# Attention scores by halves of a block: 192 key columns for 64 queries of two heads

## The chip, the core and the metric

The kernel runs on one core of a Trainium2 chip. A core has a matrix engine, TensorE (PE in the profile; PEld is its loading of weights, which overlaps the matmuls), a vector engine VectorE (DVE), an activation engine ScalarE (ACT), GpSimd (POOL), and SyncE (SP), which here issues most of the DMAs. The operands of TensorE come from the on-chip memory SBUF, its results go to banks of PSUM. Each engine works off its own queue of instructions in order; semaphores tie the queues together. The metric is the device time of one execution in microseconds; three executions of the kernel before took 1844.89, 1845.12 and 1846.22 us, so the median is 1845.12 us. The profile is of one further execution of 1844.67 us.

## The reference

Two layers of a decoder trunk on x of 1024 tokens by 1024 channels, in float32. Each layer mixes tokens (attention in a sliding window beside a causal pooling) and then runs a dense SwiGLU network; both are wrapped in norms modulated by a condition c. What matters here is the attention: 8 query heads and 2 key/value heads of 64 channels, blocks of 128 tokens, a window of 128 keys that ends at the query itself, and a sink per head that takes part in the softmax only.

```python
def sliding_window_attention_with_sinks(q, k, v, sinks):
    qb = q.reshape(B, nb, BLOCK, N_KV_HEADS, GROUP, HEAD_DIM)
    ...
    k_cat = jnp.concatenate([jnp.pad(kb, pad)[:, :-1], kb], axis=2)
    v_cat = jnp.concatenate([jnp.pad(vb, pad)[:, :-1], vb], axis=2)
    scores = jnp.einsum("bnqkgd,bnskd->bnkgqs", qb, k_cat).astype(jnp.float32)
    scores = scores * (HEAD_DIM ** -0.5)
    qi = jnp.arange(BLOCK)[:, None]
    kj = jnp.arange(2 * BLOCK)[None, :]
    diff = qi + BLOCK - kj
    ...
    valid = (diff[None] >= 0) & (diff[None] < WINDOW) & (key_abs >= 0)
    scores = jnp.where(valid[None, :, None, None], scores, NEG_INF)
    ...
    probs = jax.nn.softmax(jnp.concatenate([scores, sink], axis=-1), axis=-1)[..., :-1]
    out = jnp.einsum("bnkgqs,bnskd->bnqkgd", probs.astype(v.dtype), v_cat)
```

Query t of a block sees keys t+1 to 127 of the block before and keys 0 to t of its own block: always 128 of 256 (in block 0 only its own). Queries 0 to 63 see nothing of keys 64 to 127 of their own block, and queries 64 to 127 nothing of keys 0 to 63 of the block before.

## The kernel before

**Tiling.** The 1024 tokens are taken in two halves of 512 (T), each of four blocks of 128 (P). In each layer the combined projection comes first: u (for the pooling), q, and k with v, half by half (`u_pass`, `q_pass`, `kv_pass`), then the output projection (`mix_out`) and the feed-forward network. Operands are kept as a rounded high part and a low part (`split`, L223 on ACT for the high and L224 on DVE for the low part), so that a product takes three matmuls (`mm`, L286, is the helper of all of them; `turn`, L291, that of the transposes on TensorE).

**An attention group** is one block and one key/value head, that is 4 query heads: 16 groups per layer, 32 in the program, 4 of them in block 0. A group is a generator (`group` in `attention`) with these steps:

- Keys and queries are split into high and low parts (L1040 and L1041 for the queries), transposed on TensorE into a bank of the pool msc, and copied by ACT to sa (the transposed keys, kT in the code; L1030, L1033) and to qT (L1053, scaled). qT has one buffer.
- `att_scores` runs twice per group (u = 0, 1), each time for two heads into one bank of msc. For each head two matmuls of 256 key columns (kT's two parts) stream past 128 stationary columns, the queries of that head; in block 0 they have 128 columns.
- The 256 keys of a query are folded into 128 slots of S (the tile sb), one slot for a key of the block before or for the key of the own block at the same place: ACT copies the part of the block before (L1072), then DVE overwrites it where the key belongs to the own block's past (`copy_predicated`, L1076, with the mask own, a lower triangle). In block 0 GpSimd fills S with a large negative number in place of ACT's copy. Slot 128 holds the sink.
- The maximum (L1080, DVE), four exps with their sums (L1087, ACT), the reciprocal and the scaling (L1092 and L1093 on ACT, L1096 on DVE).
- `att_probs`: transposes of S on TensorE, split into two pth tiles (L223, L224); GpSimd's `affine_select` (L1112) makes the own block's part of each.
- `att_values`: two matmuls of pth with the difference of the two blocks' values (vz: the older values, dz: the step between blocks), added in the bank pv, and evicted by ACT and DVE (L1129, L1130).

**Order.** TensorE's order is written by hand; that of the other engines is the tile scheduler's. The groups, the pooling (`pool_mix`) and the sums that make the modulation (`ada_flow`, whose DVE part is L611 and L613) are chains woven into the dense matmuls. `weave` runs the main pass and, after each piece, steps the side chain that is due first. Due times count matmul columns issued so far, in steps of 6144 columns (STEP): a group waits LEADS[0] steps after its start, LEADS[1] after the query transposes, and so on; LEADS[4] stands between the transposes of S and the first value matmuls. CLOSE and GAPS space the modulation's sums, and a number in `gate_flow` spaces those of the gate. A dense matmul works in a pool acc of 4 banks; msc has 3, pv 1.

**Names in the prediction.** acc, msc, pv: banks of PSUM. hT: transposed input; hi, lo: the two parts of a weight (or of q and k); raw: a loaded or computed tile ahead of its split (L713 makes the normed input from a bank); uT, pt: the pooling's inputs and sums; cfa, cfb: larger tiles, of the output among others; ada: the modulation's sum; fn: a norm's tile; sk: the sinks.

Of the kernel before, what the change touches and what calls it, by code (L numbers as in the profile page):

```python
# [14 lines left out]
I32 = mybir.dt.int32  # L15
AF = mybir.ActivationFunctionType
ALU = mybir.AluOpType
# [3 lines left out]
P = 128  # L21
S = 1024
D = 1024
DEPTH = 2
NH = 8
NKV = 2
GRP = NH // NKV
HD = 64
# [7 lines left out]
NFF = DFF // P  # L36
NPAIR = NFF // 2
KD = D // P
T = 512
NT = T // P  # L40
NHALF = S // T
# [9 lines left out]
NEG = -1e30  # L51
SCALE = HD ** -0.5
# [16 lines left out]
def hybrid_decoder_kernel(  # L69
# [73 lines left out]
    def msc_bank():  # L143
# [26 lines left out]
        out=own, in_=own, pattern=[[-1, P]], compare_op=ALU.is_ge,  # L170
        fill=0.0, base=0, channel_multiplier=1,
    )

    tpos = const.tile([P, HALO], I32, name="tpos")
    nc.gpsimd.iota(tpos, pattern=[[1, HALO]], base=1, channel_multiplier=0)
# [449 lines left out]

    GATE_BEGIN = 0.0
    GATE_GAP = 1.9
    CLOSE = 1.59
    GAPS = (0.79, 0.51)

    def closing(close, got):
        yield from close(*got) or ()
# [411 lines left out]
    def att_queries_turned(stk):  # L1044

        bank = msc_bank()
        for i in range(GRP):
            turn(
                bank[:, i * P : (i + 1) * P].bitcast(F32R),
                stk[:, i].rearrange("p a d -> p (a d)"), ident_r,  # L1050
            )
        qT = t_("qT", [P, GRP * P], F32R)
        nc.scalar.activation(qT, bank, AF.Copy, scale=SCALE)  # L1053
        return qT

    def att_seen(blk):

        return slice(0 if blk else P, 2 * P)

    def att_scores(blk, u, qT, kT, S):  # L1060

        bank = msc_bank()
        cs = att_seen(blk)
        for ii in range(2):
            dst = bank[:, ii * 2 * P : (ii + 1) * 2 * P][:, cs]
            q = qT[:, (2 * u + ii) * P : (2 * u + ii + 1) * P]
            mm(dst, q, kT[0][:, cs], True, False)
            mm(dst, q, kT[1][:, cs], False, True)
        both = bank.rearrange("p (i o k) -> p i o k", i=2, o=2)
        dst = S[:, 2 * u : 2 * u + 2, 0:P]  # L1070
        if blk:
            nc.scalar.activation(dst, both[:, :, 0, :], AF.Copy)  # L1072
        else:
            nc.gpsimd.memset(dst, NEG)
        seen = own.bitcast(I32).rearrange("p (o k) -> p o k", o=1).to_broadcast([P, 2, P])
        nc.vector.copy_predicated(dst, seen, both[:, :, 1, :])  # L1076

    def att_max(S):
        mx = t_("st", [P, 8])[:, :GRP]
# [21 lines left out]
    def att_probs(blk, S):  # L1101

        bank = msc_bank()
        for i in range(GRP):
            turn(bank[:, i * P : (i + 1) * P], S[:, i, 0:P], ident)
        seen = [t_("pth", [P, 512], F32R) for _ in range(2)]
        split(*seen, bank)
        if not blk:
            return [seen]
        here = [t_("pth", [P, 512], F32R) for _ in range(2)]  # L1110
        for v, r in zip(seen, here):
            nc.gpsimd.affine_select(  # L1112
                out=r.rearrange("p (i q) -> p i q", i=GRP), in_=v.rearrange("p (i q) -> p i q", i=GRP),
                pattern=[[0, GRP], [1, P]], compare_op=ALU.is_ge, fill=0.0, base=0, channel_multiplier=-1,
            )
        return [seen, here]

    def att_values(n, vals, probs, opening, closing, cat, t):

        if opening:  # L1120
            attn["pv"] = ps.tile([P, 512], F32, tag="pv", name="pv", bufs=1)
        pv = attn["pv"]
        both = vals[:, n].rearrange("p o d -> p (o d)")
        mm(pv, both, probs[0], opening, False)
        mm(pv, both, probs[1], False, closing)
        if closing:
            high, low = (pv[o * HD : (o + 1) * HD].rearrange("p (j q) -> p j q", j=GRP) for o in range(2))
            dst = cat[n * HD : (n + 1) * HD, :, t * P : (t + 1) * P]
            nc.scalar.activation(dst, low, AF.Copy)  # L1129
            nc.vector.tensor_add(dst, high, dst)  # L1130

# [2 lines left out]
    def attention(h, qkvs, sink, cat, begin, period):  # L1134

        def group(t, n):
            blk = h * NT + t
            both = t_("sb", [P, D])
            S = both[:, : GRP * SW].rearrange("p (i k) -> p i k", i=GRP)[:, :, : P + 1]
            step = both[:, GRP * SW : GRP * SW + KVW]  # L1140
            keys = None
            if n == 0:
                if t == 0:
                    att_rotary(blk, qkvs[t], both)
                keys = att_keys(blk, qkvs[t])
            queries = att_queries(n, qkvs[t])
            if n == 0 and t + 1 < NT:
                att_rotary(blk + 1, qkvs[t + 1], both)
            if n == 0:
                if blk:  # L1150
                    nc.gpsimd.tensor_sub(step, qkvs[t][:, QK:QKV], attn["raw"])
                attn["raw"] = qkvs[t][:, QK:QKV]
            hs = slice(n * GRP, (n + 1) * GRP)
            nc.gpsimd.tensor_copy(S[:, :, P : P + 1], sink[:, hs].rearrange("p (i o) -> p i o", o=1))
            yield LEADS[0]
            if keys is not None:
                att_keys_turned(blk, keys)
            qT = att_queries_turned(queries)
            yield LEADS[1]
            kT = attn["k", blk]  # L1160
            for u in range(GRP // 2):
                att_scores(blk, u, qT, (kT[:, 2 * n], kT[:, 2 * n + 1]), S)
                if u == 0:
                    yield LEADS[2]
            att_softmax(S, att_max(S), h == 0)
            yield LEADS[3]
            probs = att_probs(blk, S)
            if n == 0:
                used = [attn["v"], att_vals("dz", step)] if blk else []
                attn["v"] = att_vals("vz", qkvs[t][:, QK:QKV])  # L1170
                attn["vals", blk] = used or [attn["v"]]
            parts = list(zip(attn["vals", blk], probs))
            for i, (vals, prob) in enumerate(parts):
                yield LEADS[4 + i]
                att_values(n, vals, prob, i == 0, i == len(parts) - 1, cat, t)

        return Chains([group(t, n) for t in range(NT) for n in range(NKV)], begin, period)

    LEADS = (0.9, 0.85, 0.25, 2.72, 1.2, 0.64)

    POOL_STEPS = len(WINDOWS) + 1

# [420 lines left out]
    def layer_rows(l, d):  # L1603
        bq = t_("bqkv", [P, QKV])
        eng = nc.sync
        eng.dma_start(bq, b_in[l : l + 1, 0:QKV].to_broadcast([P, QKV]))
        sk = t_("sk", [P, NH])
        eng.dma_start(sk, sinks[l : l + 1, :].to_broadcast([P, NH]))
        d["bq"], d["sink"] = bq, sk

    rows0 = load_col_rows(0)
# [74 lines left out]
    for l in range(DEPTH):  # L1686
# [33 lines left out]
        def gate_flow():  # L1720
            if l:
                return
            one, two = ada_gate(l, 0)
            yield from ada_flow([one], [cats[0][1][:, i, :] for i in range(4)], 3.0)
            while 1 not in cats:
                yield 0.5
            yield from ada_flow([two], [cats[1][1][:, i, :] for i in range(4)], 2.11)
# [219 lines left out]
```

## Time and profile before

| | us |
|---|---|
| median of three executions | 1845.12 |
| the profiled execution | 1844.67 |
| its span, first to last instruction | 1843.0 |
| TensorE busy | 1815.0 (98%), 8615 instructions |
| weight loads busy | 1505.1 (82%) |
| VectorE busy | 1500.5 (81%), 2450 instructions |
| ScalarE busy | 949.5 (52%), 1816 instructions |
| GpSimd busy | 76.4 (4%), 144 instructions |

The granted clock of TensorE is 0.999 of full speed on average. The rows below are the busy tenths of 40 equal slices (46 us each) of the span; attention runs in slices 2 to 7 and 21 to 26, where GpSimd works and ScalarE is busiest:

```profile
PE   7999999999999999999999999999999999999998
...
DVE  7799987787888887788976798876877887877687
ACT  4886895563222323445657759855622322344452
POOL 0022110000000000000001202100000000000000
```

The costliest group of attention's matmuls, and the loads of their stationary operand (busy us, mean ns of one, idle time ahead of them and what ended it):

```profile
L286 PEld LDWEIGHTS msc<-sa,qT 128*128 128x128 f32 x256 | 37.9, 189 | 9.3 <-ACT qT L1053 2.4 <-issue 1.6 <-ACT cfb L1195 1.2
L286 PE MATMUL msc<-sa,qT 128*128 128x256 f32 x224 | 36.5, 285 | 2.2 <-ACT qT L1053 1.0 <-DVE pth L224 0.8 <-ACT cfb L1195 0.3
```

Busy times of matmuls overlap, since one starts to stream before the one ahead of it has drained. So 285 ns is not what such a matmul costs; that is read from the distance of starts. Idle time of an engine that is not the bottleneck costs nothing by itself.

### The profile page before, as it was taken

How to read it: one execution, taken by the hardware profiler on the slowest of the kernel's cores; microseconds unless marked ns; L12 is line 12 of the kernel's file. 1: busy time of each engine (PE TensorE's matmuls, PEld its weight loads, DVE VectorE, ACT ScalarE, POOL GpSimd, SP SyncE). 2: the span in 40 equal slices, each digit the busy share in tenths (PEclk: the TensorE clock that was granted, in tenths of full speed). 3: DMA queues.
4: the chain of work that ended last, by engine and by line, in shares of the span. 5: the costliest groups of instructions: out<-in, count | busy, mean ns of one | idle time of the engine just before them, and what ended most of it. 6: DMA issues, size and time to landing. Idle time of an engine off the chain costs nothing.

```text
span 1843.0 us, 25184 instructions
## 1 busy us (share of the span) xinstructions
PE 1815.0 (98%) x8615; PEld 1505.1 (82%) x8615; DVE 1500.5 (81%) x2450; ACT 949.5 (52%) x1816; POOL 76.4 (4%) x144
## 2 busy tenths in 40 slices
PE   7999999999999999999999999999999999999998
PEld 5888888888888888888888888888888888888886
DVE  7799987787888887788976798876877887877687
ACT  4886895563222323445657759855622322344452
POOL 0022110000000000000001202100000000000000
PEclk9999999999999999999999999999999999999999
DMA  9637747764565565844577485567635545574343
GB/s 328 231 114 224 258 158 234 230 215 162 172 205 194 177 217 204 293 160 135 197 262 238 149 251 205 183 208 230 233 131 187 175 168 197 177 274 144 113 141 122
DMA packets 237157, 363.85 MB, mean 197 GB/s; under 512 B 17946, under 2 KB 126418, under 8 KB 237028
## 3 DMA queue, kind: packets, MB, share of 16 engines
q1 hardware_dynamic: 236420, 360.14, 58.9%
q10 hardware_dynamic: 576, 2.10, 0.3%
q8 instruction: 68, 1.11, 0.2%
q14 instruction: 61, 0.50, 0.1%
q0 software_dynamic: 32, 0.00, 0.0%
HBM read 274.60 MB, written 87.57 MB: 197 GB/s over the span
## 4 chain that ended last, share of the span: by engine, by line
PE 87%; ACT 6%; DVE 5%; issue 2%; DMA 1%; DVEq 0%; ACTq 0%; POOL 0%; SPq 0%; POOLq 0%
PE acc L286 80%; PE msc L286 3%; PE msc L291 2%; PE pv L286 1%; ACT raw L713 1%; ACT sb L1087 1%; DVE ada L613 1%; ACT hT L223 1%; DVE lo L224 1%; ACT hi L223 0%; ACT junk L660 0%; ACT uT L975 0%; DMA pos_i<-in_positions_dram 0%; DVE pth L224 0%; DMA cfb<-in_ada_w_dram 0%
## 5 line engine op out<-in xcount | busy, mean ns | idle before, releaser
L223 ACT ACTIVATE hi<-raw 128x1024 fp32r<-128x1024 f32 (+1 forms) x314 | 268.6, 867 | 313.0 <-PE acc L286 171.1
L224 DVE TENSOR_TENSOR lo<-raw,hi 128x1024 fp32r<-128x1024 f32 (+1 forms) x314 | 307.8, 984 | 84.9 <-ACT hi L223 82.5
L286 PE MATMUL acc<-t,hi 128*128 128x512 f32 x1056 | 325.3, 389 | 0.0
L286 PE MATMUL acc<-hT,hi 128*128 128x512 f32 x928 | 287.7, 395 | 0.0
L286 PEld LDWEIGHTS acc<-t,hi 128*128 128x128 f32 x1056 | 198.1, 188 | 41.2
L286 PE MATMUL acc<-t,lo 128*128 128x512 f32 x528 | 205.4, 389 | 0.0
L286 PE MATMUL acc<-bh,hi 128*128 128x512 f32 x520 | 202.9, 390 | 0.0
L286 PE MATMUL acc<-bh,lo 128*128 128x512 f32 x520 | 202.5, 389 | 0.0
L286 PEld LDWEIGHTS acc<-hT,hi 128*128 128x128 f32 x928 | 168.7, 188 | 31.6 <-issue 0.3
L286 PE MATMUL acc<-hT,lo 128*128 128x512 f32 x512 | 187.9, 391 | 0.0
L1396 DVE TENSOR_TENSOR fn<-acc,fn 128x512 f32<-128x512 f32 x176 | 120.5, 685 | 44.4 <-PE acc L286 44.4
L286 PE MATMUL acc<-ph,hi 128*128 128x512 f32 x328 | 126.3, 389 | 0.0
L286 PE MATMUL acc<-t,hT 128*128 128x512 f32 x528 | 123.3, 389 | 0.0
L1311 ACT ACTIVATE sb<-sb 128x512 f32<-128x512 f32 x38 | 24.0, 632 | 181.5 <-DVE sb L1396 157.3
L286 PEld LDWEIGHTS acc<-t,hT 128*128 128x128 f32 x528 | 99.1, 188 | 20.6
L286 PEld LDWEIGHTS acc<-t,lo 128*128 128x128 f32 x528 | 99.1, 188 | 20.5
L286 PEld LDWEIGHTS acc<-bh,hi 128*128 128x128 f32 x520 | 97.6, 188 | 20.2
L286 PEld LDWEIGHTS acc<-bh,lo 128*128 128x128 f32 x520 | 97.6, 188 | 20.2
L286 PEld LDWEIGHTS acc<-hT,lo 128*128 128x128 f32 x512 | 95.6, 188 | 20.0
L286 PE MATMUL acc<-b,hi 128*128 128x512 f32 x352 | 108.4, 389 | 0.0
L223 ACT ACTIVATE bh<-two_b 128x512 fp32r<-128x512 f32 x100 | 62.3, 623 | 71.7 <-PE acc L286 66.4
L286 PE MATMUL acc<-hi,hT 128*128 128x512 f32 (+1 forms) x352 | 97.4, 360 | 0.7 <-ACT hT L223 0.7
(341 smaller groups left out, 3525.5 us busy)
## 6 DMA issues: line engine op xcount, KB each, us to landing
raw<-in_w_gate_dram SPq DMA_DIRECT2D x44, 512.0 KB
raw<-in_w_up_dram SPq DMA_DIRECT2D x44, 512.0 KB
ar<-in_ada_w_dram SPq DMA_DIRECT2D x80, 256.0 KB
raw<-keeps SPq DMA_DIRECT2D x40, 512.0 KB
cfb<-in_ada_w_dram SPq DMA_DIRECT2D x72, 256.0 KB
keeps<-fn SPq DMA_DIRECT2D x66, 256.0 KB
two_b<-in_w_down_dram SPq DMA_DIRECT2D x30, 512.0 KB
raw<-in_w_in_dram SPq DMA_DIRECT2D x52, 256.0 KB
```

The costliest lines, as they stand in the source:

```text
L223: a = nc.scalar.activation(hi, src, AF.Copy)
L224: v = nc.vector.tensor_sub(lo, src, hi.bitcast(F32))
L286: return nc.tensor.matmul(dst, lhs, rhs, start=start, stop=stop)
L291: return nc.tensor.transpose(dst, src, eye_)
L613: ins = nc.vector.scalar_tensor_tensor(acc, w, c_, acc, op0=ALU.mult, op1=ALU.add)
L713: nc.scalar.activation(hf, bank, AF.Identity, bias=shift, scale=scale)
L1087: nc.scalar.activation(S[:, i, :], S[:, i, :], AF.Exp, bias=nm[:, i : i + 1], accum_out=sm[:, i : i + 1])
L1311: nc.scalar.activation(g, g, AF.Silu)
L1396: ins = nc.vector.tensor_add(halves_of(dst)[m], bank, halves_of(src)[m])
```

## The change

The queries in qT are stored by halves of the block: first the queries 0 to 63 of the four heads, then the queries 64 to 127. A stationary operand of 128 columns now holds 64 queries of two heads. Such a half sees at most 192 of the 256 keys, so each score matmul has 192 columns: keys 0 to 191 for the first half, 64 to 255 for the second (in block 0: 64 and 128 columns). Of the three runs of 64 keys in the result, ACT copies two to S (for the second half in reversed order, so that they land in their slots), and DVE's predicated copy has 64 slots per row in place of 128. In block 0 the second half needs an ACT copy of 64 slots that was not there (4 more instructions in the program). A row of S now stands for another head and query, so the sinks are loaded in two DMAs per layer, one for each half of the partitions, and copied to S another way; the select on the probabilities has a pattern of three levels, and the eviction of the values puts the queries back in order. TensorE has as many instructions as before. Four numbers that space the side chains change with it.

```diff
+HP = P // 2
...
+    nc.gpsimd.tensor_copy(own[HP:P, 0:HP], own[HP:P, HP:P])
...
-    CLOSE = 1.59
-    GAPS = (0.79, 0.51)
+    CLOSE = 1.69
+    GAPS = (0.84, 0.51)
...
         qT = t_("qT", [P, GRP * P], F32R)
-        nc.scalar.activation(qT, bank, AF.Copy, scale=SCALE)
+        nc.scalar.activation(
+            qT.rearrange("p (h i t) -> p h i t", h=2, i=GRP),
+            bank.rearrange("p (i h t) -> p h i t", h=2, i=GRP), AF.Copy, scale=SCALE,
+        )
         return qT
...
-    def att_seen(blk):
-
-        return slice(0 if blk else P, 2 * P)
-
     def att_scores(blk, u, qT, kT, S):
 
         bank = msc_bank()
-        cs = att_seen(blk)
-        for ii in range(2):
-            dst = bank[:, ii * 2 * P : (ii + 1) * 2 * P][:, cs]
-            q = qT[:, (2 * u + ii) * P : (2 * u + ii + 1) * P]
+        first = 0 if blk else P if u == 0 else HP
+        for m in range(2):
+            dst = bank[:, m * 2 * P + first : m * 2 * P + 3 * HP]
+            q = qT[:, (2 * u + m) * P : (2 * u + m + 1) * P]
+            cs = slice(u * HP + first, u * HP + 3 * HP)
             mm(dst, q, kT[0][:, cs], True, False)
             mm(dst, q, kT[1][:, cs], False, True)
-        both = bank.rearrange("p (i o k) -> p i o k", i=2, o=2)
-        dst = S[:, 2 * u : 2 * u + 2, 0:P]
+        both = bank.rearrange("p (m o k) -> p m o k", m=2, o=4)
+        dst = S[:, 2 * u : 2 * u + 2, 0:P].rearrange("p m (o k) -> p m o k", o=2)
         if blk:
-            nc.scalar.activation(dst, both[:, :, 0, :], AF.Copy)
+            nc.scalar.activation(dst, both[:, :, 0:2, :] if u == 0 else both[:, :, 1::-1, :], AF.Copy)
         else:
-            nc.gpsimd.memset(dst, NEG)
-        seen = own.bitcast(I32).rearrange("p (o k) -> p o k", o=1).to_broadcast([P, 2, P])
-        nc.vector.copy_predicated(dst, seen, both[:, :, 1, :])
+            nc.gpsimd.memset(S[:, 2 * u : 2 * u + 2, 0:P], NEG)
+            if u:
+                nc.scalar.activation(dst[:, :, 0, :], both[:, :, 1, :], AF.Copy)
+        seen = own[:, 0:HP].bitcast(I32).rearrange("p (o k) -> p o k", o=1).to_broadcast([P, 2, HP])
+        nc.vector.copy_predicated(dst[:, :, u, :], seen, both[:, :, 2, :])
...
             nc.gpsimd.affine_select(
-                out=r.rearrange("p (i q) -> p i q", i=GRP), in_=v.rearrange("p (i q) -> p i q", i=GRP),
-                pattern=[[0, GRP], [1, P]], compare_op=ALU.is_ge, fill=0.0, base=0, channel_multiplier=-1,
+                out=r.rearrange("p (h i t) -> p h i t", h=2, i=GRP),
+                in_=v.rearrange("p (h i t) -> p h i t", h=2, i=GRP),
+                pattern=[[HP, 2], [0, GRP], [1, HP]], compare_op=ALU.is_ge, fill=0.0, base=0, channel_multiplier=-1,
             )
...
-            hs = slice(n * GRP, (n + 1) * GRP)
-            nc.gpsimd.tensor_copy(S[:, :, P : P + 1], sink[:, hs].rearrange("p (i o) -> p i o", o=1))
+            last = S[:, :, P : P + 1].rearrange("p (h m) o -> p h (m o)", h=2)
+            nc.gpsimd.tensor_copy(last, sink[:, n : n + 1, :].to_broadcast([P, 2, 2]))
...
-    LEADS = (0.9, 0.85, 0.25, 2.72, 1.2, 0.64)
+    LEADS = (0.9, 0.85, 0.25, 2.72, 1.13, 0.64)
...
-        sk = t_("sk", [P, NH])
-        eng.dma_start(sk, sinks[l : l + 1, :].to_broadcast([P, NH]))
+        sk = t_("sk", [P, NH // 2])
+        for i in range(2):
+            eng.dma_start(sk[i * HP : (i + 1) * HP, :], sinks[l : l + 1, i:NH:2].to_broadcast([HP, NH // 2]))
+        sk = sk.rearrange("p (n m) -> p n m", n=NKV)
...
-            yield from ada_flow([one], [cats[0][1][:, i, :] for i in range(4)], 3.0)
+            yield from ada_flow([one], [cats[0][1][:, i, :] for i in range(4)], 2.82)
```

The numbers and the lighter copies shift the orders at some places. In the changed kernel lines stand two to seven further down (L224 becomes L226, L286 L288, L291 L293, L1076 L1080, L1080 L1084). A row names line, operation, output and inputs, and the shape of the output.

On VectorE, in the q projection of layer 0's second half (about 121 to 127 us of the span), before:

```order
L1076 COPY_PREDICATED sb<-own,msc 128x2x128
L1005 TENSOR_TENSOR vz<-qkv,vz 128x2x64
L1076 COPY_PREDICATED sb<-own,msc 128x2x128
L224 TENSOR_TENSOR pth<-msc,pth 128x512
L1080 TENSOR_REDUCE st<-sb 128x4
L1014 TENSOR_TENSOR hi<-qkv,hi 128x2x128
L1041 TENSOR_TENSOR hi<-qkv,hi 128x4x64
L224 TENSOR_TENSOR lo<-raw,hi 128x512 x2
```

The same place now:

```order
L1084 TENSOR_REDUCE st<-sb 128x4
L547 TENSOR_TENSOR ar<-msc,ar 1x512
L1232 TENSOR_TENSOR pt<-pt,rcnt 128x16
L548 TENSOR_TENSOR ar<-ar 1x512
L226 TENSOR_TENSOR lo<-raw,hi 128x512
L1094 RECIPROCAL st<-st 128x4
L1007 TENSOR_TENSOR vz<-qkv,vz 128x2x64
L1100 TENSOR_TENSOR sb<-sb,st 128x2x128
L226 TENSOR_TENSOR lo<-raw,hi 128x512
```

The two low parts of a weight stood together behind the split of probabilities and the low parts of keys and queries; now the first of them stands right behind the maximum of the group before, and those rows come after it.

On TensorE, at the second group of block 0 (about 81 to 85 us), before:

```order
L286 MATMUL msc<-sa,qT 128x128 x4
L291 MATMUL msc<-ident,sb 128x128 x4
L286 MATMUL acc<-hT,hi 128x512 x2
L286 MATMUL acc<-hT,lo 128x512
L286 MATMUL msc<-sa,qT 128x128 x4
L291 MATMUL msc<-ident,cfb 128x128 x4
```

And now:

```order
L293 MATMUL msc<-ident,sb 128x128 x4
L288 MATMUL msc<-sa,qT 128x64 x4
L288 MATMUL acc<-hT,hi 128x512 x2
L288 MATMUL acc<-hT,lo 128x512
L288 MATMUL msc<-sa,qT 128x128 x4
L293 MATMUL msc<-ident,cfb 128x128 x4
```

The transposes of the first group's probabilities (ident,sb) moved ahead of the second group's first scores.

On TensorE, near the end of the second half's u pieces (about 247 to 253 us), before:

```order
L286 MATMUL msc<-uT,pwh 128x512
L286 MATMUL msc<-lo,pwh 128x512
L286 MATMUL msc<-uT,pwl 128x512
L286 MATMUL msc<-sa,qT 128x256 x4
L291 MATMUL msc<-ident,sb 128x128 x4
```

And now:

```order
L288 MATMUL msc<-uT,pwh 128x512
L288 MATMUL msc<-lo,pwh 128x512
L288 MATMUL msc<-uT,pwl 128x512
L288 MATMUL acc<-hT,hi 128x512 x2
L288 MATMUL acc<-hT,lo 128x512
L293 MATMUL msc<-ident,hi 128x128 x4
L288 MATMUL acc<-hT,hi 128x512 x2
L288 MATMUL acc<-hT,lo 128x512
L288 MATMUL acc<-hT,hi 128x512 x2
L288 MATMUL acc<-hT,lo 128x512
L293 MATMUL msc<-ident,sb 128x128 x4
...
L288 MATMUL msc<-sa,qT 128x192 x4
```

The three pooling matmuls (uT, pwh, pwl) moved ahead of the queries' transposes (ident,hi), and the transposes of the probabilities ahead of the scores.

More of the change, by code (lines that the diff above doesn't have):

```diff
@@ L1126, in att_values @@
         if closing:
-            high, low = (pv[o * HD : (o + 1) * HD].rearrange("p (j q) -> p j q", j=GRP) for o in range(2))
-            dst = cat[n * HD : (n + 1) * HD, :, t * P : (t + 1) * P]
+            high, low = (
+                pv[o * HD : (o + 1) * HD].rearrange("p (h j q) -> p h j q", h=2, j=GRP) for o in range(2)
+            )
+            dst = cat[n * HD : (n + 1) * HD, :, t * P : (t + 1) * P].rearrange("p j (h q) -> p h j q", h=2)
             nc.scalar.activation(dst, low, AF.Copy)
```

## The prediction

> **What bounds the kernel now.** I read the page first, for the engine that sets the end, then the busy times by stretches, then what TensorE (PE) waited for. The page gives busy time and share of each engine, and the shares of the chain of work that ended last:
>
> ```profile
> PE 1815.0 (98%) x8615; PEld 1505.1 (82%) x8615; DVE 1500.5 (81%) x2450; ACT 949.5 (52%) x1816; POOL 76.4 (4%) x144
> ...
> PE 87%; ACT 6%; DVE 5%; issue 2%; DMA 1%; DVEq 0%; ACTq 0%; POOL 0%; SPq 0%; POOLq 0%
> ```
>
> PE is busy 1815.0 of 1843.0 us, so only two things can shorten the program: PE work that costs less, or some of the 28 us in which PE stands. Attention's scores are computed in two stretches only (one per layer). The windows view gives, for a stretch, its length, the busy time of PE, of the weight loads, DVE, ACT and POOL, the granted clock, the DMA share and GB/s:
>
> ```profile
> 50.00:290.00 240.00, 234.67 (x1279) 196.04 (x1278) 214.19 (x440) 191.96 (x469) 39.30 (x65) 1.00 0.59 194
> 290.00:960.00 670.00, 670.00 (x3013) 555.16 (x3012) 546.83 (x769) 290.94 (x454) 0.11 (x1) 1.00 0.61 202
> 960.00:1200.00 240.00, 237.40 (x1313) 201.15 (x1312) 198.80 (x406) 182.30 (x446) 34.30 (x66) 1.00 0.64 212
> ```
>
> Between them PE never stands (670.00 of 670.00). In the two attention stretches it stands 5.33 and 2.60 us, together 7.9 us: that is all that a lighter VectorE (DVE) or a better order can give back there. DVE is 89% and 83% busy in them, which says it can be late at single places, not that it is the bound. The waits view of PE names the places (total us, how often, the longest):
>
> ```profile
> PE msc L291 <- DVE sb L1076: 1.9, 2, 0.9
> PE acc L286 <- DVE lo L224: 1.4, 1, 1.4
> PE msc L286 <- ACT qT L1053: 1.0, 2, 0.6
> PE msc L291 <- ACT raw L713: 0.9, 2, 0.5
> PE acc L286 <- DVE fn L861: 0.9, 2, 0.6
> PE msc L286 <- DVE pth L224: 0.8, 2, 0.4
> ...
> PE msc L286 <- ACT cfb L1195: 0.3, 2, 0.2
> ```
>
> These are 7.2 of the 7.9 us, and half hang on DVE.
>
> **Term 1: the score matmuls.** In 28 of the 32 groups each of the eight score matmuls goes from 256 to 192 key columns: 224 matmuls, 56 fours. From the timeline (start, duration, times), two places with such a four among matmuls of 512 columns, at block 0 (128 columns) and later (256 columns):
>
> ```profile
> 72.04 0.56 PE L286 MATMUL msc<-sa,qT 128*128 128x128 f32 x4
> 72.44 0.68 PE L286 MATMUL acc<-hT,hi 128*128 128x512 f32 x2
> 72.95 0.39 PE L286 MATMUL acc<-hT,lo 128*128 128x512 f32 x1
> ...
> 93.69 0.63 PE L286 MATMUL msc<-sa,qT 128*128 128x256 f32 x4
> 94.16 0.63 PE L286 MATMUL acc<-hT,hi 128*128 128x512 f32 x2
> 94.63 0.40 PE L286 MATMUL acc<-hT,lo 128*128 128x512 f32 x1
> ```
>
> I go by starts, since durations overlap. Four of 128 columns with the two wide ones take 72.95 - 72.04 = 0.91 us, four of 256 with the same two 94.63 - 93.69 = 0.94 us. Half the columns save 0.03 us per four: the narrow ones sit on a floor of about 0.11 us each (0.91 less 0.47 for the two wide, by four), which the column count does not set. By columns, 192 would need three quarters of 0.47/4, 0.088 us, less than that floor. So a four of 192 costs what a four of 128 costs, and the term is 56 x 0.03 = **-1.7 us**. Bounds: 0 if 192 behaves as 256; and at the column rate of the wide ones (0.47/2/512 = 0.46 ns a column, 64 columns 0.029 us) 224 x 0.029 = -6.6 us. I take the floor because the row at 72.04 shows it with the same stationary and the same bank; the other end is a rival below. At block 0 (64 and 128 columns) the floor already holds: 0.
>
> [...]
>
> **Term 2: DVE's work.** The predicated copy goes from 2x128 to 2x64 elements a partition, 64 times. The group of the copy, and two DVE operations of one kind with 128 and 256 elements (timeline):
>
> ```profile
> L1076 DVE COPY_PREDICATED sb<-own,msc 128x256 f32<-128x256 int32 x64 | 27.6, 442 | 2.8 <-ACT sb L1072 2.6
> ...
> 120.97 0.28 DVE L1005 TENSOR_TENSOR dz<-sb,dz 128x128 fp32r<-128x128 f32 x1
> 125.37 0.41 DVE L1041 TENSOR_TENSOR hi<-qkv,hi 128x256 fp32r<-128x256 f32 x1
> ```
>
> No copy of 128 elements is in the trace. By these two it saves 0.13 us, 64 x 0.13 = 8.3 us of DVE (bounds: 0, and half of 27.6, 13.8). That is no time of the program by itself: PE's 670.00 of 670.00 shows that DVE's 82% costs nothing where nobody waits. It counts only through the waits.
>
> *The wait of 1.35 us.* PE's row, and the chain of waits (start, length, engine, tile) into it:
>
> ```profile
> 126.44 0.50 PE L286 MATMUL acc<-lo,hT 128*128 128x512 f32 x1 [1.35 <-DVE lo L224]
> ...
> 110.17 0.69 DVE pt L1220
> ...
> 114.67 0.69 DVE sb L1076 x2
> ...
> 123.79 0.68 DVE pth L224
> 124.47 0.60 DVE st L1080
> 125.07 0.38 DVE hi L1014
> 125.45 0.34 DVE hi L1041
> 125.78 0.61 DVE lo L224
> ```
>
> The weight's low part stands in DVE's queue behind a probability split (0.68), a maximum (0.60) and two low parts (0.38, 0.34). In the changed order, counted up to that instruction, these four and two predicated copies (0.69) stand behind it, and two pooling sums (0.69 each) come ahead: 1.38 - 2.69 = -1.3 us. A v split, an eviction, a scaling and a dz split also go behind it, and the 10 copies still ahead are 0.13 shorter, another -1.3. Together over 1.35, so I take the wait as gone: **-1.35**. What is late next is what now stands behind it, above all the split of the probabilities (pth), for which the waits view has 0.8 us at other places.
>
> *Block 0, twice (0.94 us each in the waits view).* PE, then ScalarE (ACT):
>
> ```profile
> 81.54 0.62 PE L291 MATMUL msc<-ident,sb 128*128 128x128 f32 x4
> 81.92 0.71 PE L286 MATMUL acc<-hT,hi 128*128 128x512 f32 x2
> ...
> 84.20 0.55 PE L291 MATMUL msc<-ident,cfb 128*128 128x128 f32 x3 [0.94 <-DVE sb L1076]
> ...
> 80.41 0.58 ACT L1053 ACTIVATE qT<-msc 128x512 fp32r<-128x512 f32 x1
> 80.89 0.76 ACT L713 ACTIVATE raw<-msc,colp 128x512 f32<-128x512 f32 x1
> ```
>
> Now the transposes of sb stand ahead of the first scores, so the cfb transposes wait for another bank, that of the probabilities' split and not that of the copy. I take half of 1.86 as gone, **-1.0** (bounds 0 and -1.9). Against it, qT now stands behind raw on ACT: 0.66 us later (its 0.76 less the overlap of 0.10 that the row before it shows, 0.58 long and 0.48 to the next start), of which the moved transposes cover 81.92 - 81.54 = 0.38: scores wait about 0.3 twice. The second scores of block 0 need an ACT copy that was not there (4 in the program); it adds to the same queue.
>
> *Around 250 and 1155 us.* PE and ACT:
>
> ```profile
> 250.73 0.74 PE L286 MATMUL msc<-sa,qT 128*128 128x256 f32 x4 [0.60 <-ACT qT L1053]
> ...
> 250.55 1.08 ACT L223 ACTIVATE hi<-raw 128x1024 fp32r<-128x1024 f32 x1
> ```
>
> There the three pooling matmuls are now issued ahead of the queries' transposes, and the scores come three wide matmuls (0.235 us each) and a set of transposes (0.38) later, 1.1 us. I take **-0.8** of the 1.0 us for qT and **-0.3** for cfb. But the 1.08 us row now stands ahead of qT on ACT and eats most of that lead, and I carry 0.4 for it among the new waits.
>
> For the other waits (raw, fn, pth and small ones, 3.35 us), nothing moves at raw; DVE being lighter is worth a quarter: **-0.8**. So the waits give -1.35 - 1.0 - 0.8 - 0.3 - 0.8 = -4.25 us. For new waits I add 2 x 0.3 at block 0 and 0.4 around 250 and 1155: **+1.0** (bounds 0 and 2 x 0.66 + 2 x 1.08 = 3.5, all of raw and all of hi uncovered at both layers).
>
> *Edits at nothing.* The sinks take one small DMA more per layer, and POOL copies them differently:
>
> ```profile
> L1154 POOL COPY sb<-sk x32: 189/445/4510, 51.4 to 1166.3; 128x4 f32<-128x4 f32 x32
> ```
>
> The first copy starts at 51.4 and takes at most 4.5 us, the first scores at 72.04: over 15 us of cover; an issue or two on SP is far below it. The longer closing times and the shorter leads move issue places only; their effect is the orders above. Evictions and the qT copy keep their element counts.
>
> **Sum.** 1844.67 (the profiled execution, 0.45 under the median of 1845.12) - 1.7 - 4.25 + 1.0 = **1839.7 us**.
>
> **Rivals.**
> (a) *The waits only move.* DVE hands its 8 us back at once: PE waits next for ACT, 80% busy in the first stretch, or for the same operands at the next place. For it: six of the seven kinds of wait are at most 0.9 us long, which one more row of 0.6 to 0.7 ahead of the operand brings back. Against it: at 126 us the queue itself is reordered. Time: only term 1 is left, 1844.67 - 1.7 = 1843.0, within 0.2%.
> (b) *Columns set the matmul.* 6.6 instead of 1.7: 1834.8. For it: a four of 256 lies on the column rate (0.47, as two of 512). Against it: the 0.91 us at block 0.
> (c) *Slower: GpSimd's select.* Its pattern gets three levels, with runs of 64. The second select of a group and the matmuls that read it:
>
> ```profile
> 135.83 0.64 POOL L1112 TENSOR_SCALAR_AFFINE_SELECT pth<-pth 128x512 fp32r<-128x512 f32 x1 [0.77 <-DVE pth L224]
> ...
> 138.90 0.61 PE L286 MATMUL pv<-pth,dz 128*128 128x512 f32 x2
> ```
>
> The reader comes 138.90 - 136.47 = 2.4 us after the end; the shorter fifth lead takes 0.07 x 6144 columns x 0.46 ns = 0.2. It decides once two selects grow by more than 2.2 us together, 0.64 to 1.75 each. At three times the duration (+2.56 a pair) each of the 28 groups with two blocks would wait 0.35: +9.8, so 1849.5. Against it: same elements, same partitions.
> (d) *The lighter copy isn't lighter* (cost per run, not per element): DVE's 8 us don't come, no wait shrinks, and term 1 and the new waits are left: 1844.67 - 1.7 + 1.0 = 1844.0.
>
> **Chances.** Forecast 0.50, (a) 0.30, (b) 0.07, (c) 0.06, (d) 0.07. The range takes the forecast with its bounds, (a), (b) and (d), from **1834.8** to **1846.0**; (c) and a little of the others lie outside. A measurement of this kernel can tell about 0.2% from no change, 3.7 us: faster means under 1841.4. Faster: 0.48 of the forecast's 0.50, all of (b), 0.03 of (a), **0.58**. Slower, over 1848.8: 0.05 of (c), 0.01 each of (a) and (d), where the new waits add up, **0.07**. Same: the rest, **0.35**.
>
> **What would show it.** Right: fours of 192 at about 0.44 us start to start; the copy at about 0.3 us; no wait for lo near 126 us; PE's standing in the two stretches near 4.7 us in place of 7.9, with scores waiting for qT at block 0. Wrong: fours near 0.35 us (b); waits of the same sum under other names (a); pv waiting for POOL's pth (c); the copy still near 0.44 us (d). The forecast fails most easily at its waits: they hang on an order that I read in rows, with durations of another execution.

## The result, and the profile after

The changed kernel takes 1871.83 us (median of 4, 1870.23 to 1872.49), the kernel before in the same comparison 1845.01 us: a ratio of 1.0144, 95% interval 1.0133 to 1.0156. It is 26.8 us slower, where 5 us less were forecast. The profiled execution took 1871.54 us, with a span of 1869.7 us. Its busy times, and the chain that ended last by engine:

```profile
PE 1824.2 (98%) x8615; PEld 1507.8 (81%) x8615; DVE 1498.8 (80%) x2450; ACT 949.9 (51%) x1820; POOL 83.2 (4%) x145
...
PE 81%; DVE 7%; ACT 7%; DMA 2%; issue 2%; POOL 0%; SPq 0%; DVEq 0%; ACTq 0%
```

DVE is busy 1.7 us less, ACT the same. PE has as many instructions and is busy 9.2 us longer, and it stands 17.5 us longer (45.5 in place of 28.0): 9.2 + 17.5 is the whole 26.7 us of span. The 17.5 us are waits; what makes the same instructions longer is read in the last section. The windows of the two attention stretches and of what lies between (columns as before):

```profile
50.00:290.00 240.00, 226.37 (x1221) 188.16 (x1220) 201.11 (x419) 182.77 (x453) 41.56 (x62) 0.98 0.56 186
290.00:960.00 670.00, 669.55 (x3011) 554.54 (x3010) 547.64 (x772) 292.94 (x457) 3.15 (x5) 1.00 0.60 199
960.00:1200.00 240.00, 229.27 (x1253) 191.59 (x1252) 187.47 (x388) 171.35 (x430) 32.14 (x62) 0.99 0.64 211
```

In the same 240 us PE now stands 13.6 and 10.7 us, where it stood 5.3 and 2.6; between the stretches hardly anything changed. DVE and ACT are *less* busy in the same 240 us than before, since attention's work is spread over a longer time: no engine became the bound. The waits of PE (total us, how often, the longest; the first row of the view, 11.6 us ahead of the program's first matmuls, where the kernel before waits 11.9 us, is left out):

```profile
...
PE msc L288 <- ACT qT L1055: 4.7, 6, 1.5
PE msc L293 <- ACT raw L715: 4.2, 3, 1.7
PE acc L288 <- DVE pth L226: 2.3, 1, 2.3
PE pv L288 <- DVE pth L226: 2.3, 3, 1.5
PE pv L288 <- POOL pth L1116: 1.8, 1, 1.8
PE msc L293 <- ACT sa L1035: 1.5, 2, 1.1
PE msc L288 <- ACT raw L715: 1.2, 2, 0.6
PE msc L293 <- ACT dz L1006: 1.2, 2, 0.7
...
```

At the places that the prediction counted, the waits are gone or small, as it said for several of them: none is left near 126 us, and at 84 us it is 0.40 us in place of 0.94. Others of the same kind, and longer, are there instead, most of them on ACT, whose work did not grow. The single operations came out as forecast. A four of score matmuls among wide ones, and the copy:

```profile
93.63 0.59 PE L288 MATMUL msc<-sa,qT 128*128 128x192 f32 x4
94.05 0.64 PE L288 MATMUL acc<-hT,hi 128*128 128x512 f32 x2
94.53 0.39 PE L288 MATMUL acc<-hT,lo 128*128 128x512 f32 x1
...
L1080 DVE COPY_PREDICATED sb<-own,msc 128x128 f32<-128x128 int32 x64 | 18.8, 297 | 4.2 <-ACT sb L1074 3.7 <-ACT sb L1078 0.3 <-issue 0.2
```

The four with two wide ones takes 94.53 - 93.63 = 0.90 us (0.94 before, 0.91 with 128 columns): the floor, not three quarters. The copy takes 297 ns (442 before). So the operations are no longer than forecast, and it is likely that the loss lies in when they are issued.

### The profile page after: what moved, and what is told of

It reads as the page before. It is cut to its first block, busy times and chain, and to the rows that moved or that the text cites. A ratio compares the mean times of both kernels' runs of the same rounds, so it can differ in the third digit from the quotient of the medians.

```text
span 1869.7 us, 25224 instructions
## 1 busy us (share of the span) xinstructions
PE 1824.2 (98%) x8615; PEld 1507.8 (81%) x8615; DVE 1498.8 (80%) x2450; ACT 949.9 (51%) x1820; POOL 83.2 (4%) x145
## 3 DMA queue, kind: packets, MB, share of 16 engines
q8 instruction: 68, 1.11, 0.2%
## 4 chain that ended last, share of the span: by engine, by line
PE 81%; DVE 7%; ACT 7%; DMA 2%; issue 2%; POOL 0%; SPq 0%; DVEq 0%; ACTq 0%
PE acc L288 74%; PE msc L288 3%; ACT sb L1091 2%; PE msc L293 2%; DMA cfb<-in_ada_w_dram 1%; PE pv L288 1%; DVE lo L226 1%; DVE ada L615 1%; DVE st L1084 1%; ACT junk L662 1%; ACT hi L225 1%; ACT raw L715 1%; DVE pth L226 0%; DVE sb L1080 0%; ACT qT L1055 0%
## 5 line engine op out<-in xcount | busy, mean ns | idle before, releaser
L226 DVE TENSOR_TENSOR lo<-raw,hi 128x1024 fp32r<-128x1024 f32 (+1 forms) x314 | 309.8, 990 | 88.1 <-ACT hi L225 82.7
L288 PE MATMUL acc<-t,hi 128*128 128x512 f32 x1056 | 325.3, 389 | 0.0
L288 PE MATMUL acc<-hT,hi 128*128 128x512 f32 x928 | 289.8, 398 | 0.0
L288 PEld LDWEIGHTS acc<-t,hi 128*128 128x128 f32 x1056 | 198.2, 188 | 41.0
L288 PE MATMUL acc<-t,lo 128*128 128x512 f32 x528 | 205.5, 389 | 0.0
L288 PE MATMUL acc<-bh,hi 128*128 128x512 f32 x520 | 203.0, 390 | 0.0
L288 PE MATMUL acc<-bh,lo 128*128 128x512 f32 x520 | 202.6, 390 | 0.0
L288 PEld LDWEIGHTS acc<-hT,hi 128*128 128x128 f32 x928 | 169.7, 190 | 31.4 <-issue 0.3
L288 PE MATMUL acc<-hT,lo 128*128 128x512 f32 x512 | 189.9, 395 | 3.4 <-DVE pth L226 2.3
L288 PE MATMUL acc<-ph,hi 128*128 128x512 f32 x328 | 126.4, 389 | 0.0
L288 PE MATMUL acc<-t,hT 128*128 128x512 f32 x528 | 123.3, 389 | 0.0
L288 PEld LDWEIGHTS acc<-hT,lo 128*128 128x128 f32 x512 | 96.9, 191 | 24.1 <-DVE pth L226 2.4
L288 PEld LDWEIGHTS acc<-t,lo 128*128 128x128 f32 x528 | 99.1, 188 | 20.7
L288 PEld LDWEIGHTS acc<-t,hT 128*128 128x128 f32 x528 | 99.1, 188 | 20.6
L288 PEld LDWEIGHTS acc<-bh,lo 128*128 128x128 f32 x520 | 97.6, 188 | 20.4
L288 PEld LDWEIGHTS acc<-bh,hi 128*128 128x128 f32 x520 | 97.6, 188 | 19.9
L288 PE MATMUL acc<-b,hi 128*128 128x512 f32 x352 | 108.4, 389 | 0.0
L288 PE MATMUL acc<-hi,hT 128*128 128x512 f32 (+1 forms) x352 | 97.1, 361 | 0.7 <-ACT hT L225 0.7
```

Of the source, the lines that this page charges most:

```text
L226: v = nc.vector.tensor_sub(lo, src, hi.bitcast(F32))
L288: return nc.tensor.matmul(dst, lhs, rhs, start=start, stop=stop)
```

## The experiments

Two theories to begin with: the loss comes from the **order** (TensorE's steps came due at other places, since score matmuls count fewer columns and four numbers changed), or from the new **operations**. In all runs below, rows of an order were compared between the built programs, with line numbers and the widened or narrowed shapes left aside.

### Operations and TensorE's order, each alone

newops_oldorder is the changed kernel with

```diff
             mm(dst, q, kT[1][:, cs], False, True)
+            issued[0] += 2 * ((2 * P if blk else P) - (3 * HP - first))
```

and the four numbers of before: TensorE's order is then that of before, row for row. oldops_neworder is the kernel before with the changed numbers and

```diff
             mm(dst, q, kT[1][:, cs], False, True)
+            issued[0] += 2 * ((192 if blk else 64 + 64 * u) - (2 * P if blk else P))
```

The other two change the four numbers alone, in the one kernel or the other.

> The changed kernel's operations with TensorE's order of before, instruction for instruction: a score matmul still counts 256 columns (128 in block 0) toward the due times, and the four numbers are those of before. Theory 1 (order): the loss comes from the places to which TensorE's steps moved, and the new operations are no dearer. It expects 1838 to 1845 us, with TensorE standing 4 to 8 us in the two attention stretches. Theory 2 (operations): the new forms themselves, the select with three levels, the rearranged copies, the extra copy and loads, make operands late. It expects 1865 to 1875 us.

> The operations of before in the changed kernel's order on TensorE: a score matmul counts 192 columns (64 and 128 in block 0), and the four numbers are the changed ones. Theory 1 (order) expects 1868 to 1885 us, at least what the changed kernel takes, since the operations are as heavy as before. Theory 2 (operations) expects 1843 to 1848 us.

> The changed kernel with the four numbers of before (CLOSE, GAPS, LEADS, the gate's gap), so that only the count of 192 columns moves TensorE's steps. Theory 1 with the numbers as the cause expects 1840 to 1848 us; theory 1 with the counted columns as the cause expects 1862 to 1880 us; theory 2 (operations) 1865 to 1875 us, as the changed kernel.

> The kernel before with the four changed numbers alone; score matmuls count 256 columns. Theory 1 with the numbers as the cause expects 1865 to 1885 us; theory 1 with the counted columns as the cause, and theory 2, expect 1843 to 1850 us.

| run | us | ratio to before, 95% interval |
|---|---|---|
| newops_oldorder | 1869.23 | 1.0134, 1.0119 to 1.0149 |
| oldops_neworder | 1861.34 | 1.0087, 1.0071 to 1.0104 |
| newops_oldnumbers | 1878.76 | 1.0182, 1.0167 to 1.0197 |
| oldops_newnumbers | 1854.17 | 1.0052, 1.0037 to 1.0067 |

Neither theory holds as it was put. With TensorE's order of before the new operations still lose 24 us; with the old operations the new order loses 16 us. The four numbers do not cause the loss: without them the changed kernel is 7 us slower still. What both theories left out is that TensorE's order alone is written by hand. The orders of ACT and DVE are the scheduler's, and it makes them anew for every program: between the kernel before and newops_oldorder 136 rows of ACT and 208 of DVE stand elsewhere, although TensorE's order is the same.

### All orders, kept or exchanged

So the orders of all engines were fixed, by an explicit dependency without a semaphore between each two neighbours of a list that was taken from the other kernel's program:

```diff
     with tile.TileContext(nc) as tc:
         hybrid_decoder_kernel(tc, *args)
+        keep_orders(tc)
...
+        for x, y in zip(row, row[1:]):
+            tc.add_manual_dep(
+                lists[engine][y], lists[engine][x].name,
+                mybir.DependencyInfo(mybir.DependencyClass.NoSync, mybir.DependencyReason.DATA),
+                reason="order on the same engine",
+            )
```

> All operations of the changed kernel, with the order of before kept on every engine: TensorE's by count and numbers as in newops_oldorder, and ScalarE's, VectorE's, GpSimd's and SyncE's by explicit dependencies without semaphores between neighbours, taken from the kernel before (the 4 extra copies, the extra mask copy and the 2 extra loads are free). Theory A (orders): the 24 us of newops_oldorder come from the orders of ScalarE and VectorE, which the scheduler made anew; expected 1838 to 1844 us, at least as fast as before, since each operation is no longer than it was. Theory B (operations): something in the new operations holds the chain up; expected 1860 to 1870 us, with the same waits (qT, raw) as newops_oldorder.

> The counterpart: the operations of before with the changed kernel's order on every engine, fixed in the same way. Theory A expects 1868 to 1880 us, as the changed kernel or some us more, since the copy and the matmuls are heavier. Theory B expects 1845 to 1862 us, no more than oldops_neworder.

newops_allorders takes 1844.57 us, ratio 1.0001 (0.9992 to 1.0009); oldops_allorders 1871.92 us, ratio 1.0145 (1.0131 to 1.0159). That settles the first question: with the orders of before, all new operations cost nothing (and gain nothing, against the 1 to 7 us that theory A hoped for); with the orders of after, the old operations lose all of it, 27 us. Within these intervals, the 26.8 us are the orders' alone: those of all engines together, TensorE's included.

### What made the orders new

narrowmm is the kernel before with narrower score matmuls (the predicated copy then reads columns that are there), narrowcopy with the shorter copy and nothing else; both leave out keys:

```diff
+            if blk:
+                dst, cs = dst[:, 0:192], slice(0, 192)
+                issued[0] += 128
...
-        nc.vector.copy_predicated(dst, seen, both[:, :, 1, :])
+        at = 64 if blk else P
+        nc.vector.copy_predicated(dst, seen, bank.rearrange("p (i c) -> p i c", i=2)[:, :, at : at + P])
```

```diff
-        seen = own.bitcast(I32).rearrange("p (o k) -> p o k", o=1).to_broadcast([P, 2, P])
-        nc.vector.copy_predicated(dst, seen, both[:, :, 1, :])
+        seen = own[:, 0:64].bitcast(I32).rearrange("p (o k) -> p o k", o=1).to_broadcast([P, 2, 64])
+        nc.vector.copy_predicated(dst[:, :, 0:64], seen, both[:, :, 1, 0:64])
```

> The kernel before, where only the score matmuls of the 28 groups behind block 0 have 192 columns in place of 256 (the last 64 keys of the block are left out, and the predicated copy reads columns that are there); the count toward the due times stays 256, so TensorE's order is that of before; the other engines' orders are the scheduler's. Theory A': the scheduler takes the narrower matmul for shorter, which it isn't on the chip (floor of 0.11 us), and lays its orders on a TensorE that is ahead of the real one: expected 1862 to 1870 us, the loss of newops_oldorder nearly whole. Theory A'' (another part, as the shorter copy, makes the orders new): 1841 to 1848 us. Theory B: 1841 to 1846 us.

> The kernel before, where only the predicated copy goes over 2x64 slots in place of 2x128 (the other 64 keys of the own block are left out). TensorE's order is that of before, the others' are the scheduler's. Theory A' expects 1842 to 1852 us: the copy moves few rows and is truly shorter on the chip. Theory A'' expects 1860 to 1870 us. Theory B expects 1838 to 1845 us.

narrowmm: 1867.44 us, ratio 1.0118 (1.0104 to 1.0132). narrowcopy: 1845.08 us, ratio 0.9999 (0.9990 to 1.0009). The matmul's width alone, with TensorE's order untouched, costs 22.7 us; the shorter copy costs nothing, and the 7.4 us less of DVE (1493.1 against 1500.5 us busy) bring nothing. Both times lie in the ranges of theory A'; whether its reason, a matmul taken for shorter, is right is the next question. How such an order hurts can be read in the timelines of ACT and PE. First the kernel before, at the queries of one group:

```profile
138.05 0.60 ACT L1053 ACTIVATE qT<-msc 128x512 fp32r<-128x512 f32 x1 [1.10 <-PE msc L291]
138.54 0.40 ACT L1087 ACTIVATE sb<-sb,st 128x129 f32<-128x129 f32 x1
...
137.49 0.46 PE L291 MATMUL msc<-ident,hi 128*128 128x128 f32 x4
...
140.42 0.64 PE L286 MATMUL msc<-sa,qT 128*128 128x256 f32 x4
```

The same place in narrowmm:

```profile
142.58 0.40 ACT L1091 ACTIVATE sb<-sb,st 128x129 f32<-128x129 f32 x1 [3.28 <-DVE st L1084]
...
144.14 0.57 ACT L1053 ACTIVATE qT<-msc 128x512 fp32r<-128x512 f32 x1
...
139.84 0.46 PE L291 MATMUL msc<-ident,hi 128*128 128x128 f32 x4
...
144.76 0.69 PE L286 MATMUL msc<-sa,qT 128*128 128x192 f32 x4 [1.82 <-ACT qT L1053]
```

In both the queries are transposed first (137.49 and 139.84). Before, qT stands ahead of another group's exps and runs at once. In narrowmm it stands behind them, and the first of them waits 3.28 us for the maximum on DVE. ACT stands idle over a copy whose input has long been there, and PE then waits 1.82 us for that copy. No operation is dearer: a queue in order has the wrong row at its head.

### Why the width makes a worse order

newops_256 is newops_oldorder with score matmuls over all 256 keys, and with copies that read their runs at the places where these then lie; mm252 is narrowmm with 252 in place of 192 (and the count made up by 8).

```diff
-        first = 0 if blk else P if u == 0 else HP
+        first = 0 if blk else P
...
-            dst = bank[:, m * 2 * P + first : m * 2 * P + 3 * HP]
+            dst = bank[:, m * 2 * P + first : (m + 1) * 2 * P]
...
-            cs = slice(u * HP + first, u * HP + 3 * HP)
+            cs = slice(first, 2 * P)
...
-        nc.vector.copy_predicated(dst[:, :, u, :], seen, both[:, :, 2, :])
+        nc.vector.copy_predicated(dst[:, :, u, :], seen, both[:, :, 2 + u, :])
```

> The changed kernel's operations except that a score matmul streams all 256 keys of the two blocks (64 of them unused), with the four numbers of before, so that TensorE's order is that of before; the other orders are the scheduler's, which now sees matmuls as long as before. Theory P (picture): the scheduler's orders are bad because it takes the 192-column matmul for shorter than the chip's; without that it lays orders as good as before: expected 1841 to 1848 us. Theory K (knife edge): any new laying-out of ScalarE's and VectorE's order loses, whatever the reason, since 44 and 133 rows move here too: expected 1858 to 1870 us.

> As narrowmm, with 252 columns in place of 192 (4 of the block's keys left out), so that to any model that goes by columns a matmul is 2 ns shorter, a sixteenth of the step of narrowmm; TensorE's order is that of before, 117 rows of ScalarE and 204 of VectorE move, more than in narrowmm. Theory P expects 1844 to 1850 us (a small error in the picture, a small loss). Theory K expects 1858 to 1870 us, as narrowmm, since as many rows move.

newops_256: 1845.87 us, ratio 1.0005 (0.9996 to 1.0014), though 44 and 133 rows stand elsewhere. mm252: 1885.17 us, ratio 1.0219 (1.0204 to 1.0235). Theory K falls with the first and theory P with the second: the matmul that is nearest to 256 columns loses most. The orders give the hint. Rows that move against the kernel before, by the width of the score matmuls behind block 0, with TensorE's order the same in all:

| columns | 256 | 252 | 192 | 128 | 72 | 64 | 60 |
|---|---|---|---|---|---|---|---|
| rows of ACT | 0 | 117 | 86 | 64 | 23 | 0 | 2 |
| rows of DVE | 0 | 204 | 177 | 165 | 67 | 0 | 9 |

At 64 columns no row of any engine moves, as at 256. From these rows I estimate that the scheduler takes the one for as long as the other, that is, each column of a narrower matmul for four: a matmul would then be longer in its picture than before by 4 x 252 - 256 = 752, 512 and 256 columns' time at 252, 192 and 128. This is read out of the orders; how the scheduler counts is not shown.

mm128 is narrowmm with 128 columns (and the copy reading columns 0 to 127).

> As narrowmm and mm252, with 128 columns (half of the keys left out); 64 rows of ScalarE and 165 of VectorE move, TensorE's order is that of before. Theory Q (the scheduler takes a matmul of under 256 columns for four times as long per column, so 252 columns for 752 columns longer than before, 192 for 512, 128 for 256, and 64 for no longer, where indeed no row moves): the loss grows with that error, 40 us at 252 and 22 at 192, so 6 to 15 us here, 1851 to 1860 us. Theory K (any rearranged row costs): 20 us and more, 1865 to 1885 us. Theory P (the picture goes by columns, so 128 is a larger error than 192): over 22 us, above 1867 us.

mm128: 1854.12 us, ratio 1.0046 (1.0032 to 1.0061), 9.4 us more, in the range of theory Q alone. Losses of 40, 23 and 9 us for estimated errors of 752, 512 and 256 columns go with the error, not with the columns. At these three widths they go with the number of moved rows as well; but newops_oldorder, also with 192 columns, moves more rows than mm252 (136 and 208 against 117 and 204) and loses 24 us, not 40, and newops_256 moves 177 and loses nothing. On the chip, 192 columns cost less than 256 (0.90 against 0.94 us above). If the scheduler believes TensorE slower at each of 224 matmuls, it would put what waits for TensorE, as qT, too far back; this last step is argued, not shown.

### The waits that were left

Both kernels are newops_allorders with rows of the kept lists moved, no other edit.

> newops_allorders (all new operations, the orders of before kept) with 13 rows of the two orders moved by hand, at seven places where TensorE still waits there: at 84 and 993 us the predicated copy ahead of the low part lo and hT; at 126 the two low parts lo ahead of the maximum and of hi; at 203 and 1108 the probabilities' low part pth ahead of the rotary's product; at 80 qT and the two scalings ahead of hT on ScalarE; at 235 and 1140 raw ahead of the second uT; at 250 and 1155 qT ahead of a copy cfa, and cfb ahead of hi. The waits there sum to 1.35 + 2 x 0.78 + 1.41 + 2 x 0.44 + 2 x 0.38 + 2 x 0.58 + 2 x 0.21 = 7.5 us in newops_allorders. Theory A (each wait is the place of one row in a queue): 4 to 7 us come back, 1837.5 to 1841 us. Rival (the waits only move, ScalarE and VectorE being 80% busy there): 1842 to 1848 us.

> newops_tuned with six more rows moved, at the places where that run's trace has TensorE waiting: at 90 us the low part lo ahead of hT on VectorE (2.2 us, followed by matmuls at half their rate), at 137 the eviction cfa ahead of the low part of pt (0.9), at 246 the queries' hi ahead of raw on ScalarE and ahead of the maximum on VectorE (0.7), at 274 and 1178 pth ahead of hi (0.4 each). Theory A (each wait is the place of one row): 1838 to 1842 us. Rival (waits only move): 1843 to 1847 us.

newops_tuned: 1845.74 us, ratio 1.0006 (0.9997 to 1.0014). newops_tuned2: 1844.31 us, ratio 0.9998 (0.9989 to 1.0007). The rival was right both times. PE's standing in the two stretches, from the windows of newops_allorders and of newops_tuned2:

```profile
50.00:290.00 240.00, 233.95 (x1281) 195.54 (x1280) 210.77 (x439) 192.15 (x473) 39.49 (x65) 1.00 0.60 196
...
960.00:1200.00 240.00, 237.12 (x1315) 200.62 (x1314) 194.36 (x405) 182.76 (x448) 34.36 (x66) 1.00 0.65 209
```

```profile
50.00:290.00 240.00, 234.92 (x1277) 194.39 (x1276) 210.23 (x438) 191.31 (x470) 40.62 (x65) 1.00 0.61 195
...
960.00:1200.00 240.00, 238.04 (x1319) 201.32 (x1318) 194.87 (x406) 182.72 (x448) 35.18 (x66) 1.00 0.65 212
```

Some twenty rows moved, at places worth some 12 us in the two traces that named them, and the standing went from 8.9 to 7.0 us. That is not in the time either: PE is busy 1815.5 us in newops_tuned2, 1.5 us longer than in newops_allorders. The waits in the first stretch, before the moves (newops_allorders) and after them (newops_tuned2):

```profile
PE msc L288 <- ACT qT L1055: 2.1, 2, 1.4
PE acc L288 <- DVE lo L226: 1.4, 1, 1.4
PE msc L293 <- DVE sb L1081: 0.8, 1, 0.8
...
```

```profile
PE pv L288 <- DVE pth L226: 1.1, 1, 1.1
PE msc L293 <- DVE hi L1016: 0.7, 1, 0.7
PE msc L288 <- ACT qT L1055: 0.6, 1, 0.6
PE msc L293 <- ACT sa L1035: 0.5, 1, 0.5
PE msc L293 <- DVE sb L1101: 0.4, 1, 0.4
...
```

Most of the named waits went, and others stand at other places. A few stayed: raw at 235 and 1140 us (0.24 us, where it was 0.38), cfb at 251 us, and the wait at 137 us, 0.91 us for cfa in newops_tuned, is one of 1.11 us for pth now. No version was found that is faster than the kernel before.

## Why the prediction was wrong

The sign was wrong, and 32 us lie between forecast and result (1871.5 of the profiled execution less 1839.7).

- **Term 1, the matmuls:** right in its mechanism, and of the right size where a four was measured: -1.7 us forecast; 0.04 us by the rows above, -2.2 us if all 56 fours are like that one. As time of the program it did not come: with the orders of before (newops_allorders) PE is busy 1814.0 us against 1815.0, and the time is the same. The floor shows in the whole group too: the median start-to-start distance of the 192-column matmuls is 0.112 us, that of the 256-column ones in the kernel before 0.119 us, where columns alone would give 0.75 x 0.119 = 0.089 us. By the rows, rival (b) is out: columns alone would have given 0.82 us for the four with its two wide ones, where 0.90 were measured.
- **Term 2, DVE's work:** its size was right (0.145 us a copy, 0.13 forecast), and so was the warning that it is no time by itself: narrowcopy, where it stands alone, is at 0.9999. In the changed kernel DVE as a whole is busy only 1.7 us less.
- **The waits, -4.25 us:** wrong. The wait for lo at 126 us did go in the changed kernel, and others on ACT and DVE came. The reading ahead of it was off as well: of the 7.2 us of waits shown, 5.0 hang on DVE, not half. newops_tuned and newops_tuned2 show it in the small: rival (a), to which 0.30 was given, is what removing waits does here.
- **New waits, +1.0 us with an upper bound of 3.5:** the step that failed, by more than all others together. It priced two places, "2 x 0.3 at block 0 and 0.4 around 250 and 1155", and its bound came from the same two. The order of the whole stretch was new: 252 rows of ACT and 359 of DVE stand elsewhere in the changed kernel. I read three places, took the rest for as good as it was, and took a changed order for a few rows with a price each. Measured: 16.4 us more standing in the two windows, where the waits and the new waits together were to give 3.25 us less. The sum also had no term for a longer busy time of PE, which came to 9.2 us, most of it right behind the longest new waits (last section).
- **"The longer closing times and the shorter leads move issue places only; their effect is the orders above":** the effect is larger than the forecast (oldops_newnumbers +9.2 us), though in the changed kernel they help (newops_oldnumbers is 7 us worse than the changed kernel).
- **Rival (c), GpSimd's select:** the form is not the cause. The median went from 635 to 662 ns; its one wait of 1.8 us comes from a select of 5.77 us, and oldops_neworder, with the old form, has one of 5.95 us.

What stays open: that the scheduler takes a column of a narrower matmul for four is my estimate from the rows that moved at seven widths, not shown. What each moved row costs was not measured one by one.

## What to carry to other kernels

Where a scheduler orders some engines and a person others, a change of an operation's shape can also change the orders that the scheduler makes (86 rows of ACT and 177 of DVE in narrowmm, with TensorE's order untouched); compare all engines' orders before pricing a saving, and where hundreds of rows move, a good order may go with them (252 and 359 rows and 27 us here, though 44 and 133 rows cost nothing in newops_256). A kernel with numbers that space its side chains holds an order, not only operations: keep that order by explicit dependencies and the operations can be judged alone (newops_allorders, 1.0001). And a queue worked off in order makes a wait out of one misplaced row (3.28 us on ACT and 1.82 us on PE in narrowmm), so that taking single waits away can move them to other places, as in newops_tuned and newops_tuned2.

## What was not expected of the hardware

Behind four waits of 1.63 to 2.29 us in the changed kernel, matmuls run at about half their rate, at a granted clock of 0.50, for 3.41 us. The timeline of PE at the first of them:

```profile
166.09 0.50 PE L288 MATMUL pv<-pth,dz 128*128 128x512 f32 x1 [1.83 <-POOL pth L1116]
166.43 0.40 PE L288 MATMUL acc<-hi 128*128 128x512 f32 x1
166.67 0.39 PE L288 MATMUL acc<-lo,hi 128*128 128x512 f32 x1
...
167.93 0.63 PE L288 MATMUL acc<-hi,uT 128*128 128x512 f32 x1
168.35 0.63 PE L288 MATMUL acc<-hi 128*128 128x512 f32 x1
...
170.49 0.45 PE L288 MATMUL acc<-hi,uT 128*128 128x512 f32 x1
170.78 0.39 PE L288 MATMUL acc<-hi 128*128 128x512 f32 x1
```

From 166.43 the starts are 0.24 us apart, from 167.93 to 170.49 they are 0.43 (six in 2.56 us), and then 0.29; the granted clock of the two attention windows is 0.98 and 0.99, where it was 1.00. The granted clock falls to 0.50 four times there. The windows of these stretches (columns as before, the granted clock third from the end):

```profile
167.18:170.59 3.41, 3.41 (x10) 2.65 (x9) 3.29 (x6) 2.02 (x5) 0.00 (x0) 0.50 0.75 264
211.55:214.96 3.41, 3.41 (x10) 2.92 (x11) 3.24 (x17) 0.38 (x1) 0.79 (x2) 0.50 0.94 384
249.10:252.51 3.41, 3.02 (x12) 2.11 (x11) 2.26 (x3) 3.18 (x7) 0.58 (x2) 0.50 0.22 82
1167.29:1170.70 3.41, 3.00 (x9) 2.56 (x10) 1.94 (x4) 3.18 (x7) 1.32 (x2) 0.50 0.06 24
```

They begin 0.03 to 2.03 us after the ends of waits of 1.83, 2.29, 1.66 and 1.63 us, the four longest of the two attention stretches (at 1167 us a further wait, of 1.09 us, still runs as the stretch begins). PE is busy in them for 12.84 us and at half the rate loses half of that, an estimated 6.4 us. So a third of the loss (9.2 of 26.7 us of span) is not standing, and most of that third stands right behind the longest waits. The waits next in length do not have it: in the 4 us behind 1.51 us for qT (to 146.52) and behind 1.49 us for pth (to 111.53) the granted clock is 1.00. What of a wait brings the half rate is not shown.
